# Up projections of a ConvGLU feed-forward: nine feature tiles by seven products instead of six, their weight sums loaded three and summed two tiles ahead, x's differences written earlier in the program

## Chip, cores and metric

The kernel runs on one core of one Trainium2 chip. The metric is the device time of one execution in microseconds (us). An execution was also recorded by the hardware profiler; times "at" a point below are microseconds from the start of that recorded span.

## What is computed

One encoder block on a sequence of 512 tokens with 1024 features. Three mixers (a bidirectional mLSTM, neighbourhood attention, cross-attention into a memory) are projected from a normed x, gated, merged and added to x. Then comes the feed-forward part, where the change lies:

```python
def conv_glu_ffn(h, w_up, w_conv, b_conv, w_down):
    a, u = jnp.split(h @ w_up, 2, axis=-1)
    return (jax.nn.gelu(dwconv3(a, w_conv, b_conv)) * u) @ w_down

x = x + merged @ w_out[l]
x = x + conv_glu_ffn(rms_norm(x, ffn_norm_g[l]), w_ffn_up[l], w_ffn_conv[l], b_ffn_conv[l], w_ffn_down[l])
return rms_norm(x, final_norm_g)
```

`D_FF` is 2816, so a and u have 22 feature tiles of 128 each. `dwconv3` is a convolution of three taps along the tokens.

## The kernel before

Features lie on the 128 partitions, tokens on the free axis. Every matmul of a float32 product is made of three in a rounded format: high part by high part, high by low, low by high (`mm3`, L370 to L372). So each weight block is split before use: ScalarE copies it into the rounded format (the high part, L336), VectorE subtracts that from it (the low part, L337). Blocks come in a fixed order: `emit_raw` (L246) loads them into a ring of three `wr` buffers from SP's queue, three blocks ahead, and the halves of a block are split one block ahead into four `w` buffers.

The stage before is the output projection: for each of 8 feature tiles an x tile is loaded (L1314, SP), 24 matmuls run, VectorE adds x (x2, L1316), ScalarE and VectorE split the scaled sum into `HH` and `HL`, ScalarE squares it (L1322), and GpSimd (POOL in the profile) adds the squares into `acc2` (L1323).

From `acc2` a chain makes `rb`, the row of reciprocal roots of the mean squares, on all partitions: a transposition on VectorE (L177), four stores of `td` to DRAM (L180), a load of `U` (L186), a sum and a scaling on VectorE (L202, L203), a power on POOL (L204), a small transposition (L205), four stores of `rd` (L208) and a broadcast load of `rb` (L210). Up to that point the up projections work on x2 without the root; `conv` (L570) multiplies tile after tile by `rb` first.

The up stage is a loop over f, 22 feature tiles:

- A plain tile makes a and u with two projections, `pa` and `pu`, of 24 matmuls of 512 columns each. Tiles 0 and 1 are run ahead of their convolutions; tile 1's results stand in the other pool of PSUM banks (`at`).
- A tile in `SUP` is made by seven products. With the tokens in two halves, the contraction tiles in even and odd, and the weights in a and u, a 2 by 2 block product needs eight products of half width; `up_seven` needs seven, each of 4 x 3 matmuls of 256 columns, in the order `UP_ORDER`. Their factors are blocks of x and of the weights or sums and differences of two (`FORMS`). The plain blocks come as one `ub` load; product 1's difference of weights is made on VectorE (L1383); for products 4, 7, 3 and 6 one addend is loaded into a `ut` buffer by SP (`up_load`, L1366) and the other is added to it in flight by a DMA from POOL's queue (`up_sum`, L1374). `up_weight` splits each of them (L1390, L1391).
- `x_forms(p)` makes the differences of x for one pair of contraction tiles: two copies on ScalarE (L1338), three subtractions on VectorE (L1341 to L1343), a split (L1345 to L1347). Its buffers y and d are single.

Behind the matmuls of a tile: multiplication by `rb` and the three taps (L570, L572 to L574), gelu on ScalarE (L1451), multiplication by `rb` again on POOL (`c`, L1453), and c times u on VectorE (L1467 or L1469). Tiles 0 to 11 end in `ur`, which the down projection uses in its own seven-product form; tiles 12 to 21 are split into `UH` and `UL`. In tiles 3 to 10, x2 is transposed and stored (`turn_out`), and in tiles 6 to 13 loaded back (`turn_in`) as the residual of the down projection.

A scheduler in the framework sets each engine's order of instructions from the written program, so an engine's order isn't the order of the text. `in_turn` chains an instruction behind the one before it on its engine. From an engine's queue instructions run in order; a DMA that waits for its buffer holds up those behind it in the same queue. The large buffers (`unit`, 14 of them), the small ones (`E`, six) and others are taken from pools when free.

## Time and profile before

| | |
|---|---|
| time, median of 3 runs | 851.85 us (851.35 to 852.55) |
| the profiled execution's own time | 851.33 us |
| its span | 849.6 us |
| granted TensorE clock, mean | 0.999 |
| busy: TensorE, its weight loads, VectorE, ScalarE, POOL | 841.0, 716.3, 622.4, 476.4, 175.6 us |
| moved by DMA | 147.32 MB, 173 GB/s |
| up projections | about 494.7 to 731.2 |
| tiles 2, 3, 4 / 5 / 6 / 7 start | 516.5, 527.4, 539.8 / 550.8 / 560.8 / 571.7 |
| down projections start | 731.2 |

PE is TensorE, PEld its weight loads, which run beside matmuls; DVE is VectorE, ACT ScalarE, SPq the queue of DMA issues on SP. A row of the order of time gives start, duration, engine, source line, operation and tiles (written <- read), and in brackets how long the engine stood idle before it and what ended that. Most waits of engines other than TensorE cost nothing by themselves.

### The profile page before, as it was taken

What the parts mean: (1) busy time and instruction counts of PE and PEld (TensorE: products, weight loads), DVE (VectorE), ACT (ScalarE), POOL (GpSimd) and SP (SyncE); (2) the same over time, 40 slices, a digit from 0 to 9 for tenths busy, and PEclk for the clock granted to TensorE, in tenths of its full rate; (3) what the DMA queues carried; (4) which work ended last, traced back from release to release, by engine and by line L of the source; (5) the groups of instructions that cost most, each with busy time, mean ns of one, the idle gap of its engine ahead of it and who ended that gap; (6) DMA issues with size and microseconds to landing.
All of it is one profiled execution on the core that took longest, in us unless ns stands there. A gap on an engine that the chain in (4) does not pass through costs nothing.

```text
span 849.6 us, 12743 instructions
## 1 busy us (share of the span) xinstructions
PE 841.0 (99%) x4214; PEld 716.3 (84%) x4214; DVE 622.4 (73%) x1246; ACT 476.4 (56%) x992; POOL 175.6 (21%) x268
## 2 busy tenths in 40 slices
PE   9999999999999999999999999999999999999997
PEld 8898988888888888888888888799999888888885
DVE  6699777766458748998676666877777856687893
ACT  7465557775446548888644644444455544444562
POOL 2000200000101840454000121423332111320421
PEclk9999999999999999999999999999999999999999
DMA  8236736563425856788743343588886333895882
GB/s 273 84 114 202 246 120 205 168 198 102 145 90 172 229 145 199 223 250 234 232 140 109 117 159 99 132 235 226 224 229 147 101 109 124 234 231 143 250 197 99
DMA packets 86226, 147.32 MB, mean 173 GB/s; under 512 B 11784, under 2 KB 38920, under 8 KB 86160
## 3 DMA queue, kind: packets, MB, share of 16 engines
q1 hardware_dynamic: 71600, 127.47, 46.9%
q0 software_dynamic: 14272, 18.90, 12.2%
q8 instruction: 33, 0.54, 0.3%
q14 instruction: 33, 0.27, 0.1%
q10 hardware_dynamic: 288, 0.14, 0.1%
HBM read 130.84 MB, written 15.62 MB: 172 GB/s over the span
## 4 chain that ended last, share of the span: by engine, by line
PE 91%; DMA 3%; DVE 2%; issue 2%; ACT 1%; POOL 0%; SPq 0%; POOLq 0%; DVEq 0%; ACTq 0%
PE mm L372 23%; PE mm L370 23%; PE mm L371 23%; PE at L372 6%; PE at L371 6%; PE at L370 6%; DMA s<-xT 2%; PE at L1033 1%; PE at L866 1%; PE at L868 1%; PE at L850 1%; DVE w L337 1%; PE at L404 0%; PE at L999 0%; PE at L1000 0%
## 5 line engine op out<-in xcount | busy, mean ns | idle before, releaser
L370 PE MATMUL mm<-u,w 128*128 128x512 f32 x763 | 298.8, 392 | 0.0
L372 PE MATMUL mm<-u,w 128*128 128x512 f32 x763 | 297.5, 390 | 1.0 <-DVE w L337 1.0
L371 PE MATMUL mm<-u,w 128*128 128x512 f32 x763 | 297.5, 390 | 0.0
L337 DVE TENSOR_TENSOR w<-wr,w 128x512 fp32r<-128x512 f32 (+2 forms) x233 | 159.8, 690 | 69.9 <-ACT w L336 68.5
L336 ACT ACTIVATE w<-wr 128x512 fp32r<-128x512 f32 (+2 forms) x232 | 144.8, 627 | 113.0 <-PE mm L372 72.2
L372 PEld LDWEIGHTS mm<-u,w 128*128 128x128 f32 x763 | 143.4, 188 | 32.0 <-DVE w L337 1.8
L371 PEld LDWEIGHTS mm<-u,w 128*128 128x128 f32 x763 | 143.5, 188 | 28.6
L370 PEld LDWEIGHTS mm<-u,w 128*128 128x128 f32 x763 | 143.5, 188 | 28.5
L679 POOL DMA_DIRECT2D u<-nav_d x128 | 62.3, 505 | 99.8 <-PE at L1033 52.3
L270 POOL TENSOR_TENSOR s<-s,rb 128x512 f32<-128x512 f32 x21 | 31.1, 1480 | 154.4 <-ACT s L1451 151.0
L372 PE MATMUL at<-u,w 128*128 128x256 f32 (+1 forms) x200 | 60.2, 301 | 0.0
L371 PE MATMUL at<-u,w 128*128 128x256 f32 (+1 forms) x200 | 60.0, 300 | 0.0
L370 PE MATMUL at<-u,w 128*128 128x256 f32 (+1 forms) x200 | 60.0, 300 | 0.0
L270 ACT ACTIVATE w<-u 128x512 fp32r<-128x512 f32 x52 | 32.7, 632 | 41.5 <-PE mm L372 20.6
L370 PE MATMUL mm<-w,u 128*128 128x512 f32 x128 | 50.4, 394 | 0.0
L372 PE MATMUL mm<-w,u 128*128 128x512 f32 x128 | 49.9, 390 | 0.0
L371 PE MATMUL mm<-w,u 128*128 128x512 f32 x128 | 49.9, 390 | 0.0
L270 DVE TENSOR_TENSOR w<-u,w 128x512 fp32r<-128x512 f32 x52 | 35.7, 688 | 18.1 <-ACT w L270 17.5
L572 ACT ACTIVATE s<-pad,vec 128x512 f32<-128x512 f32 x30 | 24.3, 812 | 27.6 <-DVE pad L570 24.3
L371 PEld LDWEIGHTS at<-u,w 128*128 128x128 f32 x200 | 38.2, 191 | 1.5
L370 PEld LDWEIGHTS at<-u,w 128*128 128x128 f32 x200 | 38.2, 191 | 1.5
L372 PEld LDWEIGHTS at<-u,w 128*128 128x128 f32 x200 | 38.2, 191 | 1.3
(333 smaller groups left out, 1390.3 us busy)
## 6 DMA issues: line engine op xcount, KB each, us to landing
wr<-wflat SPq DMA_DIRECT2D x118, 512.0 KB, 3.7
u<-wflat SPq DMA_DIRECT2D x50, 256.0 KB, 5.7
td<-s SPq DMA_DIRECT2D x172, 64.0 KB, 1.9
U<-td SPq DMA_DIRECT2D x41, 256.0 KB, 4.0
s<-xT SPq DMA_DIRECT2D x24, 256.0 KB, 4.0
ut<-wflat SPq DMA_DIRECT2D x24, 256.0 KB, 4.3
ut<-wflat POOLq DMA_DIRECT2D x24, 256.0 KB, 7.3
u<-wflat POOLq DMA_DIRECT2D x24, 256.0 KB, 7.6
```

The source lines that it names most:

```text
L270: chain[eng] = getattr({"V": V, "A": A, "G": G}[eng], what)(*a, **k).ins
L336: A.activation(h[:, u:v], src, AF.Copy)
L337: V.tensor_tensor(l[:, u:v], src, h[:, u:v].bitcast(F32), op=ALU.subtract)
L370: PE.matmul(ps, lh, rh, start=start, stop=False)
L371: PE.matmul(ps, lh, rl, start=False, stop=False)
L372: st["mm"] = PE.matmul(ps, ll, rh, start=False, stop=stop).ins
L572: A.activation(t1, pad[:, 0:512], AF.Identity, scale=vcol(w, i), bias=vcol(b, i))
L679: G.dma_start(vw[r * 32:(r + 1) * 32, i * 256:(i + 1) * 256], nav_v[hf, r, CW[b]:CW[b] + 32, hp * 256:(hp + 1) * 256])
L850: PE.matmul(pv[:, i, 0:129], kt[:, d, i], va[:, i + d, h, 0:129], start=True, stop=True)
L866: PE.matmul(pv[:, d, 0:129], E[J // 2][:, 2 * (J % 2) + d, :], va[:, J, h, 0:129], start=True, stop=not inter)
L868: PE.matmul(pv[:, d, 0:129], Q[d][:, i, :], C[:, d, i, 0:129], start=False, stop=True)
L1033: PE.matmul(py[:, bl * 256:(bl + 1) * 256], vw[:, c:c + P], pp[bl][:, hf * 256:(hf + 1) * 256], start=hf == 0, stop=hf == 1)
```

## The change

Tiles 3, 17 and 19 join `SUP`. `up_load` runs three tiles ahead (tile 3's own at tile 0), `up_sum` two tiles ahead (tile 3's behind rb's chain in the text). The last of the four `ut` buffers comes from another tag, so six `E` buffers hold two tiles' sums. Products 7, 3 and 6 write banks of the `mm` pool. `x_forms` is written ahead: block 0 inside the output projection, 1 to 3 between tiles 0 and 1. The residual's way back moves from tiles 6 to 13 into tiles 20 and 21, into `unit` buffers; tiles 12 to 15 put `UH` and `UL` into the buffers that it leaves. `in_turn` covers the power of rb's chain, rb's load and the `ut` loads too.

```diff
-SUP = (5, 7, 9, 11, 13, 15)
+SUP = (3, 5, 7, 9, 11, 13, 15, 17, 19)
...
-        G.tensor_tensor(col[:, :NT], v, nhalf[:, :NT], op=ALU.pow)
+        in_turn("G", "tensor_tensor", col[:, :NT], v, nhalf[:, :NT], op=ALU.pow)
...
-        SY.dma_start(rb, d.partition_broadcast(P))
+        in_turn("S", "dma_start", rb, d.partition_broadcast(P))
...
     def x_forms(p):
 
+        for q in (p, 4):
+            if q not in xf:
+                xf[q] = unit(F32R)
...
+    for f in range(KT):
+        xr = scr()
+        chain["S"] = SY.dma_start(xr, xT[:, f, :]).ins
+        ps = proj(("out", f), GH, GL)
...
+            chain["G"] = G.tensor_tensor(acc2, acc2, sq, op=ALU.add).ins
+        if f == 3:
+            x_forms(0)
...
-                r = tp.tile([P, S], F32, tag="E", name=nm("ut"), bufs=EB)
-                SY.dma_start(r, src[:, :HC])
+                tag, n = ("nab", 2) if i == 6 else ("E", EB)
+                r = tp.tile([P, S], F32, tag=tag, name=nm("ut"), bufs=n)
+                in_turn("S", "dma_start", r, src[:, :HC])
...
-        b12, b45, b7, b36 = [atps() for _ in range(4)]
+        b12, b45, b7, b36 = atps(), atps(), mmps(), mmps()
...
         if f == 0:
+            up_load(SUP[0])
...
             t2 = turn_in(turn_out(by4(acc2)), "nab", 2)
+            x_forms(1)
...
             pa1 = proj(("ua", 1), HH, HL, bank=atps)
+            x_forms(2)
             rb2 = rstd_row_turned(t2, "2")
+            up_sum(SUP[0])
+            x_forms(3)
             pu1 = proj(("uu", 1), HH, HL, bank=atps)
         elif f in SUP:
+            if f + 2 in SUP:
+                up_sum(f + 2)
             pa, pu = up_seven(f)
         else:
-            if f + 1 in SUP:
-                up_sum(f + 1)
             pa = pa1 if f == 1 else proj(("ua", f), HH, HL)
-        if f + 2 in SUP:
-            up_load(f + 2)
+        if f + 3 in SUP[1:]:
+            up_load(f + 3)
...
-        if f < KT // 2:
-            x_forms(f)
...
-            if f % 2 == 0:
-                ou.append(unit(F32R))
...
+            if f < 2 * NSP + 4:
+                for tag, part in zip("HR", (UH, UL)):
+                    part.append(tp.tile([P, S], F32R, tag=tag, name=nm("UH"), bufs=4))
...
-        if 6 <= f < 14:
-            t, g = (f - 6) % NT, (f - 6) // NT
-            res[t, g] = turn_in(turns[t, g], "HR"[g], 4)
+        if f >= FT - 2:
+            g, u = FT - 1 - f, unit()
+            for t in range(NT):
+                q = u[:, t * S:(t + 1) * S]
+                SY.dma_start(q, turns[t, g])
+                res[t, g] = q.rearrange("p (i s a) -> p s i a", i=4, a=32)
```

VectorE around tile 2's convolution, before. `pad_150` and `s_5565` belong to tile 2, `u_5336` is d of `x_forms`, `w_5584` the second half of tile 3's first weights, `u_5335` holds products c times u:

```order
L573 SCALAR_TENSOR_TENSOR s_5565<-pad_150,vec,s_5565 128x512
L1346 TENSOR_TENSOR u_5339<-u_5336,u_5339 128x768
L1347 TENSOR_TENSOR u_5342<-u_5336,u_5339 128x512
L574 SCALAR_TENSOR_TENSOR s_5565<-pad_150,vec,s_5565 128x512
L1341 TENSOR_TENSOR u_5336<-u_5337 128x512
L1342 TENSOR_TENSOR u_5336<-u_5337 128x512
L1343 TENSOR_TENSOR u_5336<-u_5337 128x256
L337 TENSOR_TENSOR w_5584<-wr_5466,w_5584 128x512
L1467 TENSOR_TENSOR u_5335<-mm_5587,s_5565 128x512
```

The same place now. `s_5601` is tile 2's convolution, `wr_5510` tile 3's block of plain weights, `s_5609` the difference for its first product, `w_5611` and `w_5614` its first two splits, `ut_5348` a sum:

```order
L570 TENSOR_TENSOR pad_150<-mm_5567,rb_5495 128x512
L1390 TENSOR_TENSOR s_5609<-wr_5510 128x512
L1478 TENSOR_TENSOR u_5347<-mm_5373,s_5544 128x512
L1478 TENSOR_TENSOR u_5347<-at_5518,s_5552 128x512
L573 SCALAR_TENSOR_TENSOR s_5601<-pad_150,vec,s_5601 128x512
L1398 TENSOR_TENSOR w_5611<-s_5609,w_5611 128x512
L574 SCALAR_TENSOR_TENSOR s_5601<-pad_150,vec,s_5601 128x512
L1398 TENSOR_TENSOR w_5614<-wr_5510,w_5614 128x512
L1398 TENSOR_TENSOR w_5653<-ut_5348,w_5653 128x512
```

No difference of x stands there any more; the splits of tile 3's first products do.

VectorE between the transposition of `acc2` (L177, two rows above the first one here) and rb's scaling (L203), now; `u_5009` is d, `w` rows are splits, L202 is rb's sum. Before, only L202 and four splits stood between L177 and L203:

```order
L1328 TENSOR_TENSOR u_5009<-u_5010 128x256
L1331 TENSOR_TENSOR u_5473<-u_5009,u_5473 128x768
L1332 TENSOR_TENSOR u_5174<-u_5009,u_5473 128x512
L1326 TENSOR_TENSOR u_5009<-u_5010 128x512
L337 TENSOR_TENSOR w_5369<-wr_5308,w_5369 128x512
L1327 TENSOR_TENSOR u_5009<-u_5010 128x512
L1328 TENSOR_TENSOR u_5009<-u_5010 128x256
L337 TENSOR_TENSOR w_5442<-wr_5356,w_5442 128x512
L202 TENSOR_REDUCE y_5482<-U_5423 128x4
L1331 TENSOR_TENSOR u_5501<-u_5009,u_5501 128x768
L337 TENSOR_TENSOR w_5445<-wr_5356,w_5445 128x512
L203 TENSOR_SCALAR y_5482<-y_5482 128x4
```

Blocks 2 and 3 of the differences moved in here.

POOL behind the power of rb's chain (L204), before: four multiplications c times rb (tiles 0 to 3), then the sums of tile 5:

```order
L204 TENSOR_TENSOR y_5452<-y_5451,nhalf 128x4
L1453 TENSOR_TENSOR s_5500<-s_5500,rb_5464 128x512
L270 TENSOR_TENSOR s_5516<-s_5516,rb_5464 128x512
L270 TENSOR_TENSOR s_5565<-s_5565,rb_5464 128x512
L270 TENSOR_TENSOR s_5655<-s_5655,rb_5464 128x512
L270 DMA ut_5646<-wflat 128x512
```

and now, the power being the first row (`ut_5348` to `ut_5354` are tile 3's):

```order
L270 TENSOR_TENSOR y_5483<-y_5482,nhalf 128x4
L270 DMA ut_5348<-wflat 128x512
L270 DMA ut_5350<-wflat 128x512
L270 DMA ut_5352<-wflat 128x512
L270 DMA ut_5354<-wflat 128x512
L270 TENSOR_TENSOR s_5544<-s_5544,rb_5495 128x512
```

The sums of tile 3 moved between the power and the first multiplication.

More of the change, by code (lines that the diff above doesn't have):

```diff
@@ L269, in in_turn @@
         with tc.issue_after(chain[eng]) if eng in chain else ExitStack():
-            chain[eng] = getattr({"V": V, "A": A, "G": G}[eng], what)(*a, **k).ins
+            chain[eng] = getattr({"V": V, "A": A, "G": G, "S": SY}[eng], what)(*a, **k).ins
     def emit_sum(i):
@@ L1347, in x_forms @@
         V.tensor_tensor(xf[4][:, p * S:(p + 1) * S], d[:, 3 * M:], h[:, 3 * M:].bitcast(F32), op=ALU.subtract)
+    for f in range(KT):
+        xr = scr()
+        chain["S"] = SY.dma_start(xr, xT[:, f, :]).ins
+        ps = proj(("out", f), GH, GL)
+        V.tensor_tensor(x2[f], ps, xr, op=ALU.add)
+        split_act(HH[f], HL[f], x2[f], vcol("ffn_g", f))
+        if f == 0:
+            A.activation(acc2, x2[f], AF.Square)
+        else:
+            sq = scr()
+            A.activation(sq, x2[f], AF.Square)
+            chain["G"] = G.tensor_tensor(acc2, acc2, sq, op=ALU.add).ins
+        if f == 3:
+            x_forms(0)
+    x2v = [u[:, :4 * S].rearrange("p (f s) -> p f s", f=4) for u in x2u]
+    ur[0] = unit()
+    ur.extend(unit() for _ in range(NSP // 2 - 3))
+    ou, UH, UL = [], [], []
+    res, turns = {}, {}
     def x_of(i, p):
@@ L1392, in up_weight, with up_first @@
         uw[f, "w", i] = h, l
+    def up_first(f):
+        uw[f] = split.pop(BINDEX["ub", f][0])
+        for n in range(2):
+            up_weight(f, n)
     def up_seven(f):
-        b12, b45, b7, b36 = [atps() for _ in range(4)]
+        b12, b45, b7, b36 = atps(), atps(), mmps(), mmps()
         at = {1: b12[:, :M], 2: b12[:, M:], 4: b45[:, :M], 5: b45[:, M:], 7: b7[:, :M], 3: b36[:, :M], 6: b36[:, M:]}
@@ L1460, in hybrid_block @@
                 ws = weights(("uu", f))
-                uw[f + 1] = split.pop(BINDEX["ub", f + 1][0])
-                for n in range(2):
-                    up_weight(f + 1, n)
+                up_first(f + 1)
                 split[BINDEX["uu", f][0]] = ws
```

36 lines of the change are left out of this document (10 added, 26 removed).

## The prediction

> **What bounds the kernel now.** I read the page first (busy shares, then the chain that ended last), and after that the order of time on TensorE through the up projections, with a table by stretch.
>
> ```profile
> span 849.6 us, 12743 instructions
> PE 841.0 (99%) x4214; PEld 716.3 (84%) x4214; DVE 622.4 (73%) x1246; ACT 476.4 (56%) x992; POOL 175.6 (21%) x268
> ...
> PE 91%; DMA 3%; DVE 2%; issue 2%; ACT 1%; POOL 0%; SPq 0%; POOLq 0%; DVEq 0%; ACTq 0%
> ```
>
> TensorE carries 91% of the chain. So the time changes by what TensorE has to issue, plus the places where it waits. Busy time does not show the first, since matmuls overlap; the distance from one start to the next does. These rows of the order of time are the first matmul of up tile 2 (516.48), a pause in tile 3, and the first matmuls of tiles 5, 6, 7 and 8. Columns: start, duration, engine, line.
>
> ```profile
> 516.48 0.39 PE L370 MATMUL mm<-u,w 128*128 128x512 f32 x1
> ...
> 530.30 0.39 PE L371 MATMUL mm<-u,w 128*128 128x512 f32 x1
> 531.74 0.50 PE L372 MATMUL mm<-u,w 128*128 128x512 f32 x1 [1.05 <-DVE w L337]
> ...
> 550.76 0.28 PE L370 MATMUL at<-u,w 128*128 128x256 f32 x1
> 560.84 0.40 PE L370 MATMUL mm<-u,w 128*128 128x512 f32 x1
> 571.74 0.28 PE L370 MATMUL at<-u,w 128*128 128x256 f32 x1
> 581.82 0.40 PE L370 MATMUL mm<-u,w 128*128 128x512 f32 x1
> ```
>
> A plain tile (6) takes 571.74 - 560.84 = 10.90 us for 48 matmuls of 512 columns, 0.227 us each. A tile by seven products (7) takes 581.82 - 571.74 = 10.08 us for 84 matmuls of 256 columns, 0.120 us each. The difference is only 0.82 us: seven products save an eighth of the columns, and shorter matmuls give more than a third of that back.
>
> ```profile
> 560.84:571.74 10.90, 10.90 (x50) 9.01 (x49) 8.88 (x15) 3.66 (x6) 5.14 (x5) 1.00 0.83 229
> 571.74:581.82 10.08, 10.08 (x85) 10.07 (x84) 7.58 (x14) 6.62 (x13) 1.30 (x1) 1.00 1.02 278
> 665.90:731.20 65.30, 65.30 (x290) 54.09 (x289) 42.65 (x63) 29.16 (x46) 8.73 (x7) 1.00 0.39 128
> ```
>
> By stretch (columns: stretch, length, then busy time and count of PE, PEld, DVE, ACT, POOL, the granted clock, DMA share, GB/s), the six plain tiles 16 to 21 take 65.30/6 = 10.88 us each, so the plain tile's price holds late too. VectorE is busy 16.5 us of a pair's 20.98 and DMA over 0.8: both are near their limits, but neither stops TensorE in these rows.
>
> **The change, part by part.**
>
> *Three more tiles by seven products (3, 17, 19).* 3 x 0.82 = 2.46 by the pair above; with 10.88 for the plain tile 2.40. I take **-2.4**. Moving two of the four banks to the other pool changes no matmul; tile 2's and 4's banks come free at their convolution and product, long before the fifth product asks. VectorE and ScalarE take on what the pair above shows them carrying without a stop, so this work costs nothing there; if that cover were gone, each split that is late would cost its own 0.7 us.
>
> *A rule that speaks against it.*
>
> ```profile
> L370 PEld LDWEIGHTS mm<-u,w 128*128 128x128 f32 x232 | 43.6, 188 | 8.9
> ...
> L370 PEld LDWEIGHTS at<-u,w 128*128 128x128 f32 x184 | 35.2, 191 | 0.8
> ```
>
> A seven-product tile has 84 weight loads of 191 ns against 48 of 188, and its loads leave no idle time (0.8 us in 184). If they could not run beside matmuls, 84 x 0.191 = 16.0 us of loads against 48 x 0.188 = 9.0 would make such a tile 16.0 - 9.0 = 7.0 us dearer in loads alone. The starts 0.120 us apart say that they do overlap. The Trainium skill, "TensorE: Matmul & The Clock Gate", section "What overlaps and what doesn't" under "The mechanism", says that a load overlaps running matmuls only where the row groups differ; this trace disagrees, and I keep it as a rival of one chance in a hundred.
>
> *The pause in tiles 2 to 4 goes.* From 516.48 to 550.76 are 34.28 us for three plain tiles of 10.90, so 1.58 us are lost, nearly all at 531.74. There TensorE waits for the low half of tile 3's weights (L337), which VectorE makes late:
>
> ```profile
> 529.47 0.68 DVE L1341 TENSOR_TENSOR u<-u 128x512 f32<-128x512 f32 x1
> 530.07 0.68 DVE L1342 TENSOR_TENSOR u<-u 128x512 f32<-128x512 f32 x1
> 530.67 0.41 DVE L1343 TENSOR_TENSOR u<-u 128x256 f32<-128x256 f32 x1
> 531.00 0.68 DVE L337 TENSOR_TENSOR w<-wr,w 128x512 fp32r<-128x512 f32 x1
> ```
>
> Three differences of x stand right ahead of it. In the changed order all four blocks of differences stand ahead of the first convolution, and this split does not exist any more. **-1.6**.
>
> *What is late next: the first weights of tile 3.* Seven products now start where tile 3 started, at 516.48 + 2 x 10.90 = 527.38, and its third matmul (527.6) needs the low half of the block's own difference. Its place on VectorE is behind the convolutions of tiles 0, 1 and 2, and these begin only when the row of reciprocal roots (rb) has landed:
>
> ```profile
> 518.46 0.69 DVE L570 TENSOR_TENSOR pad<-mm,rb 128x512 f32<-128x512 f32 x1 [3.15 <-DMA rb<-rd]
> ...
> 526.06 0.69 DVE L1467 TENSOR_TENSOR u<-at,s 128x512 f32<-128x512 f32 x1 [0.57 <-POOL s L270]
> 526.67 0.74 DVE L573 SCALAR_TENSOR_TENSOR s<-pad,vec,s 128x512 f32<-128x512 f32 x1
> 527.33 0.95 DVE L1346 TENSOR_TENSOR u<-u,u 128x768 fp32r<-128x768 f32 x1
> 528.20 0.68 DVE L1347 TENSOR_TENSOR u<-u,u 128x512 fp32r<-128x512 f32 x1
> ```
>
> As many VectorE rows stand between that L570 and tile 2's L573 as before, so the latter comes 526.67 - 518.46 = 8.2 us after rb; the split follows 0.66 us later (L573's distance to the row behind it, 527.33) and takes 0.68. It ends at rb + 9.5. So **TensorE waits (rb's landing - 518.1)**. With rb as before that is 0.4 us. Where does rb land?
>
> ```profile
> 499.79 1.30 POOL L1323 TENSOR_TENSOR acc<-acc,s 128x512 f32<-128x512 f32 x1 [4.06 <-ACT s L1322]
> 501.12 0.71 DVE L177 STREAM_TRANSPOSE s<-acc 128x512 f32<-128x512 f32 x1 [1.21 <-POOL acc L1323]
> 507.86 0.69 DVE L202 TENSOR_REDUCE y<-U 128x4 f32<-128x512 f32 x1 [1.39 <-DMA U<-td]
> 509.07 0.16 DVE L203 TENSOR_SCALAR y<-y 128x4 f32<-128x4 f32 x1
> 510.62 1.31 SPq L208 DMA_DIRECT2D rd<-y  x4
> 515.11 0.34 SPq L210 DMA_DIRECT2D rb<-rd  x1
> ```
>
> This chain starts at the last output tile, which waits for its x (loaded by SP at 494.03), and that load stands behind a weight load that waits for VectorE:
>
> ```profile
> 492.30 0.68 DVE L1316 TENSOR_TENSOR u<-mm,s 128x512 f32<-128x512 f32 x1
> 492.90 0.67 DVE L337 TENSOR_TENSOR w<-wr,w 128x512 fp32r<-128x512 f32 x1
> 494.03 0.37 SPq L1314 DMA_DIRECT2D s<-xT  x1
> 497.67 0.69 DVE L1316 TENSOR_TENSOR u<-mm,s 128x512 f32<-128x512 f32 x1 [1.39 <-PE mm L372]
> ```
>
> Differences prepared sooner take rows from in front of 492.30. Stepping through the new order from the fourth output tile on with 3.6 us from an x load's issue to use (494.03 to 497.67) and 1.3 us of VectorE behind each sum, the last one comes at 495.3, 2.4 us sooner. Half of that goes again: between transposition and L202 there are now nine rows of differences and splits, about 5.1 us at their distances in the rows above, and some 1.2 us of waiting for ScalarE, so L202 is not at 505.5 but at about 506.1; and one more row of differences (0.87, from L1346 to L1347 above) stands between L202 and L203. Net rb 0.9 us sooner.
>
> Against it: the four weight sums of tile 3 now stand on POOL directly behind the power (L204), so their 1 MB moves while rd and rb do. No row shows rb beside sums. The nearest are the small writes td beside them (first row, 540 to 560) and with less of them (585 to 607), median us to landing last:
>
> ```profile
> td<-s SPq DMA_DIRECT2D x8, 64.0 KB, 6.8
> ...
> td<-s SPq DMA_DIRECT2D x11, 64.0 KB, 1.8
> ```
>
> That is 0 to 5.0 us; a gain is excluded, since nothing is taken from these queues. rd has 0.5 KB and rb 256 KB, the four td 256 KB in far smaller pieces, so I take 2.0, under half. Then rb lands at 518.46 - 0.9 + 2.0 = 519.6 and the wait is **+1.5**; its ends are 0 (no contention) and 4.5 (5.0). The Trainium skill, "DMA: Bandwidth & Descriptors", section "Queues, rings and completion order", says that a DMA engine takes turns between queues packet by packet. By that rule rb meets at most as much foreign data as it has itself, 256 KB, about 1 us at the 260 GB/s that the table below shows, and the wait would be 0.5; the td row went beyond such a share, so I do not lower the sum.
>
> *Loads three and sums two tiles ahead.* ScalarE's waits for sums cost TensorE nothing in the trace, so their end is worth 0. On POOL the four issues pass one multiplication each; c is due a product later, 0 again.
>
> *x2's way back (2 MB) moves from tiles 6 to 13 into tiles 20 and 21,* on SP ahead of late raw weights.
>
> ```profile
> U<-td SPq DMA_DIRECT2D x41, 256.0 KB, 4.0
> ...
> 710.00:715.00 5.00, 5.00 (x24) 4.14 (x23) 2.67 (x4) 1.61 (x3) 0.32 (x1) 1.00 0.18 52
> 735.00:740.00 5.00, 5.00 (x24) 4.14 (x23) 2.81 (x5) 2.21 (x4) 1.78 (x2) 1.00 1.07 254
> ...
> 742.19 0.63 ACT L270 ACTIVATE w<-u 128x512 fp32r<-128x512 f32 x1 [1.99 <-DMA u<-wflat]
> ```
>
> At 254 GB/s the 2.1 MB take 8 us, and the DMA share of 0.18 at 710 has room, but four raw blocks move from about 720 to 730, into a stretch that is full (1.07), where ScalarE already waits 1.99 us. TensorE reaches that block, the tenth of the down projection, behind seven sums of 6 matmuls and two plain blocks of 12, at 731.2 + 66 x 0.227 = 746.2; its split is done some 1.3 us after 742.19, so 2.7 us are to spare. I take **0**; the ends are 0 and 4.
>
> **Sum**, against the profiled execution's own 851.33 (span 849.6): 851.33 - 2.4 - 1.6 + 1.5 = 848.8. The median of the runs is 851.85, 0.5 above, so **849.4**.
>
> **Rivals.**
> - *No wait at tile 3:* rb sooner, or sums that do not slow it. 848.8 - 1.5 + 0.5 = 847.8. For it: the two DMAs are small. Chance 0.17, faster.
> - *A new wait for the one removed:* rb 0.8 to 4.2 us later than I take it, a wait of 2.3 to 5.7 us, 850.2 to 853.5. For it: the td row's 5.0. 0.21, same.
> - *Slower by that one mechanism:* it decides where the wait passes 4.0 + 1.7 = 5.7 us, that is where rb lands after 523.8, 6.2 us of contention against the chain's own sooner start. At 6.5 us of wait 854.4. For it: both rd and rb pass beside sums, one after the other; against it their size. 0.06.
> - *The down projection starts short of weights:* 1 to 3.5 us, about 851.9, same, 0.07; over 4 us, 853.8, slower, 0.04. For it the 1.07; against it that the 2.7 us to spare.
> - *It does nothing* (tiles held by VectorE, 16.5 us of 20.98): 851.85, 0.02. *Weight loads bind:* three tiles 7.0 us dearer instead of 0.8 cheaper, 849.4 + 2.4 + 21 = about 873, 0.01.
>
> **How the numbers follow.** The forecast (wait 0.7 to 2.3 us) has 0.42. 0.2% of 851.85 is 1.7 us, about what a measurement tells from no change, so faster means below 850.15 and slower above 853.55. Faster 0.42 + 0.17 = 0.59; same 0.21 + 0.07 + 0.02 = 0.30; slower 0.06 + 0.04 + 0.01 = 0.11. The range, 847.4 to 852.8, leaves out the slower cases and the ends of the best and the late one. The forecast's own range is 848.5 to 850.2.
>
> **What would show it.** Nine tiles of 10.1 us on TensorE; no pause of 1.4 us within 48 matmuls of 512 columns; a pause of about 1.5 us at the third matmul of tile 3, ended by VectorE's split; L570 first at about 519.6, with rd and rb slower than 3.3 us to land. I am wrong if rb lands before 518 or after 521, if TensorE stops between tile 4 and 21, or if it stops between 731 and 760 for a split that waited for a DMA.

## The result and the profile after

| | before | after |
|---|---|---|
| median of 20 runs each, us | 851.84 (850.27 to 853.25) | 853.52 (852.47 to 855.02) |
| profiled execution, us (its span) | 851.33 (849.6) | 853.43 (851.7) |
| mean granted TensorE clock in it | 0.999 | 0.995 |

The ratio is 1.0021, with a 95% interval of 1.0015 to 1.0028: the change costs 1.3 to 2.4 us. Predicted were 849.4, with a range of 847.4 to 852.8.

The first page of after, its span, its busy times and the shares of the chain of work that ended last:

```profile
span 851.7 us, 13056 instructions
...
PE 839.9 (99%) x4322; PEld 720.2 (85%) x4322; DVE 640.5 (75%) x1276; ACT 484.5 (57%) x1010; POOL 187.7 (22%) x280
...
PE 92%; DMA 3%; issue 2%; DVE 1%; POOL 1%; ACT 0%; SPq 0%; POOLq 0%; DVEq 0%; ACTq 0%
```

Nothing on it looks wrong. TensorE is even busy 1.1 us less than before, and the time is 2 us longer. That can only be idle time or a stretch at another rate, so I looked for it in the order of time on TensorE (start, duration, engine, line): the first matmul of tile 2, the last of tile 2, the first three of tile 3, the first of tile 4 and the first of tile 5.

```profile
515.76 0.39 PE L370 MATMUL mm<-u,w 128*128 128x512 f32 x1
...
526.68 0.39 PE L372 MATMUL mm<-u,w 128*128 128x512 f32 x1
529.80 0.58 PE L370 MATMUL at<-u,w 128*128 128x256 f32 x1 [2.74 <-ACT w L1397]
530.18 0.42 PE L371 MATMUL at<-u,w 128*128 128x256 f32 x1
532.18 0.58 PE L372 MATMUL at<-u,w 128*128 128x256 f32 x1 [1.58 <-DVE w L1398]
...
544.00 0.40 PE L370 MATMUL mm<-u,w 128*128 128x512 f32 x1
...
554.91 0.28 PE L370 MATMUL at<-u,w 128*128 128x256 f32 x1
```

All of the loss lies in tile 3. From 515.76 to 544.00 are 28.24 us for two tiles that need 10.91 + 10.07 = 20.98 by the table below; 7.3 us are lost. Tile 2 ends at 526.9, so the third matmul of tile 3, the first that needs the low half of its weights (L1398), was due at 526.9 + 2 x 0.12 = 527.15 and came 5.0 us later. Another 2.0 are rate: 82 matmuls from 532.18 to 544.00 take 11.82 us, 0.144 each, where 0.120 each would take 9.84. (The last 0.25 are lost within tile 2.) The table by stretch (length, busy time and count of PE, PEld, DVE, ACT and POOL, then granted clock, DMA share, GB/s) says why:

```profile
528.00:530.00 2.00, 0.20 (x1) 0.20 (x2) 1.60 (x2) 1.44 (x3) 2.00 (x2) 0.92 0.00 0
530.00:532.00 2.00, 0.60 (x2) 0.30 (x2) 1.82 (x3) 0.79 (x2) 0.14 (x1) 0.50 0.00 0
532.00:534.00 2.00, 1.82 (x8) 1.82 (x9) 1.99 (x4) 1.15 (x2) 0.47 (x1) 0.50 0.00 0
534.00:536.00 2.00, 2.00 (x12) 2.00 (x11) 1.99 (x2) 0.63 (x1) 2.00 (x3) 0.50 0.40 127
536.00:538.00 2.00, 2.00 (x16) 2.00 (x16) 0.96 (x3) 0.98 (x3) 2.00 (x3) 0.87 0.62 95
538.00:540.00 2.00, 2.00 (x19) 2.00 (x18) 1.70 (x3) 1.15 (x3) 0.67 (x1) 1.00 1.06 245
```

The granted clock halves 2.6 us after tile 2's last matmul has ended (527.07; from the share of 0.92 it falls at 529.7), and it is still at half when TensorE has work again: 12 matmuls in two microseconds instead of 19. Before had a stop of 1.05 us at this place, and its clock stayed up.

Everywhere else the kernel does what was expected of it. The same table over the start of the down projection, a plain tile and a tile by seven products:

```profile
733.60:760.00 26.40, 26.40 (x118) 21.84 (x117) 19.43 (x31) 14.05 (x23) 9.06 (x11) 1.00 0.98 270
544.00:554.91 10.91, 10.91 (x50) 9.02 (x49) 9.49 (x16) 4.87 (x8) 2.29 (x2) 1.00 0.74 217
554.91:564.98 10.07, 10.07 (x85) 10.07 (x84) 7.38 (x13) 5.68 (x11) 4.45 (x5) 1.00 0.82 181
```

What is tile 3 late for? VectorE's rows (the first multiplication by rb, and the low half of tile 3's first weights), SP's and POOL's issues, and the transfers between 505 and 525 (the queues' share of 16 engines; issues with KB each and median us to landing):

```profile
522.56 0.69 DVE L570 TENSOR_TENSOR pad<-mm,rb 128x512 f32<-128x512 f32 x1 [7.97 <-DMA rb<-rd]
...
531.44 0.68 DVE L1398 TENSOR_TENSOR w<-s,w 128x512 fp32r<-128x512 f32 x1
```

```profile
511.27 3.57 POOL L270 DMA_DIRECT2D ut<-wflat  x4
```

```profile
511.58 1.31 SPq L208 DMA_DIRECT2D rd<-y  x4
512.93 0.36 SPq L246 DMA_DIRECT2D wr<-wflat  x1
515.27 0.34 SPq L270 DMA_DIRECT2D rb<-rd  x1
515.66 2.46 SPq L270 DMA_DIRECT2D ut<-wflat  x4
```

```profile
q1 hardware_dynamic: 1292, 3.09, 46.4%
q0 software_dynamic: 576, 1.05, 32.2%
...
ut<-wflat POOLq DMA_DIRECT2D x4, 256.0 KB, 9.0
ut<-wflat SPq DMA_DIRECT2D x4, 256.0 KB, 8.6
rb<-rd SPq DMA_DIRECT2D x1, 256.0 KB, 7.3
```

rb needs 7.3 us where before it landed 518.46 - 515.11 = 3.35 us after its issue, and VectorE waits for it for 7.97 us. The split then ends 9.6 us behind rb. The raw weight block issued on SP ahead of rb (512.93) is late as well: it takes 7.6 us to land, at 520.5.

### The profile page after: what moved, and what is told of

Read it like the earlier page. It is cut to its first block, busy times and chain, and to the rows that moved or that the text cites. A ratio compares the mean times of both kernels' runs of the same rounds, so it can differ in the third digit from the quotient of the medians.

```text
span 851.7 us, 13056 instructions
## 1 busy us (share of the span) xinstructions
PE 839.9 (99%) x4322; PEld 720.2 (85%) x4322; DVE 640.5 (75%) x1276; ACT 484.5 (57%) x1010; POOL 187.7 (22%) x280
## 4 chain that ended last, share of the span: by engine, by line
PE 92%; DMA 3%; issue 2%; DVE 1%; POOL 1%; ACT 0%; SPq 0%; POOLq 0%; DVEq 0%; ACTq 0%
PE mm L370 23%; PE mm L371 23%; PE mm L372 23%; PE at L372 6%; PE at L371 5%; PE at L370 5%; PE at L1033 1%; DMA s<-xT 1%; DMA rb<-rd 1%; PE at L866 1%; PE at L868 1%; PE at L850 1%; DMA ut<-wflat 1%; PE at L999 0%; PE at L1000 0%
## 5 line engine op out<-in xcount | busy, mean ns | idle before, releaser
L370 PE MATMUL mm<-u,w 128*128 128x512 f32 (+1 forms) x823 | 310.5, 377 | 0.0
L372 PE MATMUL mm<-u,w 128*128 128x512 f32 (+1 forms) x823 | 309.2, 376 | 0.0
L371 PE MATMUL mm<-u,w 128*128 128x512 f32 (+1 forms) x823 | 309.2, 376 | 0.0
L337 DVE TENSOR_TENSOR w<-wr,w 128x512 fp32r<-128x512 f32 (+2 forms) x221 | 151.0, 689 | 57.4 <-ACT w L336 55.8
L336 ACT ACTIVATE w<-wr 128x512 fp32r<-128x512 f32 (+2 forms) x220 | 137.1, 626 | 83.1 <-PE mm L372 54.3
L372 PEld LDWEIGHTS mm<-u,w 128*128 128x128 f32 x823 | 155.0, 188 | 28.4 <-DVE w L337 0.4
L371 PEld LDWEIGHTS mm<-u,w 128*128 128x128 f32 x823 | 155.1, 188 | 26.6
L370 PEld LDWEIGHTS mm<-u,w 128*128 128x128 f32 x823 | 155.1, 188 | 26.5
L270 POOL TENSOR_TENSOR s<-s,rb 128x512 f32<-128x512 f32 x22 | 33.2, 1512 | 157.6 <-ACT s L1469 157.6
L370 PE MATMUL at<-u,w 128*128 128x256 f32 (+1 forms) x176 | 54.3, 309 | 2.7 <-ACT w L1397 2.7
L372 PE MATMUL at<-u,w 128*128 128x256 f32 (+1 forms) x176 | 54.3, 308 | 1.6 <-DVE w L1398 1.6
L371 PE MATMUL at<-u,w 128*128 128x256 f32 (+1 forms) x176 | 54.1, 308 | 0.0
L370 PEld LDWEIGHTS at<-u,w 128*128 128x128 f32 x176 | 34.7, 197 | 4.7 <-ACT w L1397 3.2
L370 PE MATMUL mm<-w,u 128*128 128x512 f32 x96 | 37.8, 394 | 0.0
L372 PE MATMUL mm<-w,u 128*128 128x512 f32 x96 | 37.4, 390 | 0.0
L371 PE MATMUL mm<-w,u 128*128 128x512 f32 x96 | 37.4, 389 | 0.0
L372 PEld LDWEIGHTS at<-u,w 128*128 128x128 f32 x176 | 34.5, 196 | 3.1 <-DVE w L1398 1.9
L371 PEld LDWEIGHTS at<-u,w 128*128 128x128 f32 x176 | 34.6, 197 | 1.6
```

Source lines behind the costliest of these rows:

```text
L270: chain[eng] = getattr({"V": V, "A": A, "G": G, "S": SY}[eng], what)(*a, **k).ins
L336: A.activation(h[:, u:v], src, AF.Copy)
L337: V.tensor_tensor(l[:, u:v], src, h[:, u:v].bitcast(F32), op=ALU.subtract)
L370: PE.matmul(ps, lh, rh, start=start, stop=False)
L371: PE.matmul(ps, lh, rl, start=False, stop=False)
L372: st["mm"] = PE.matmul(ps, ll, rh, start=False, stop=stop).ins
```

## The experiments

Three theories. **A**: POOL's four sums of tile 3 (software queue, 1 MB), which move at the same time as rd and rb, make rb late; the first weights of tile 3 stand behind the convolutions on VectorE and are late with it. **B**: tile 5's four loads, issued right behind rb on the same queue, make it late. **C**: rb is not decisive; VectorE has too much to do there. And one question of size: how much of the loss is the clock?

Each kernel was timed beside before on the same chip, and the differences below are ratios times 851.8. Edits are against the changed kernel unless another is named.

**1. Tile 3's loads and sums moved into the output projection** (the two functions are defined earlier for it).

```diff
     for f in range(KT):
...
+        if f == 0:
+            up_load(SUP[0])
+        if f == 4:
+            up_sum(SUP[0])
...
         if f == 0:
-            up_load(SUP[0])
...
-            up_sum(SUP[0])
             x_forms(3)
```

> Tile 3's loads and POOL's four sums move from beside rb to the output projection; the four loads of tile 5 stay right behind rb on SP. Theory A (POOL's sums slow rb): rb lands 3.4 us after its issue instead of 7.3, TensorE waits at most 1 us at tile 3, the granted clock stays at 1.00, time 847.5 to 848.5. Theory B (the loads behind rb slow it): rb still takes about 7 us and the time stays at 853.5. Theory C (VectorE's added work makes the weights late whatever rb does): rb may land sooner, the first split of tile 3 still ends near 532, time 853 or so.

Measured: 854.86 us, ratio 1.0036 (1.0024 to 1.0049). rb's own time fell, from 7.3 to 5.1 us, but rb landed no sooner, at 523.02. The reason is the same collision at another place: the sums now move beside an x load of the output projection. In this kernel that x load was issued at 486.44, and VectorE got it at

```profile
494.13 0.69 DVE L1357 TENSOR_TENSOR u<-mm,s 128x512 f32<-128x512 f32 x1 [5.47 <-DMA s<-xT]
```

7.7 us later; in after the same load was issued at 485.55 and used at

```profile
489.86 0.69 DVE L1338 TENSOR_TENSOR u<-mm,s 128x512 f32<-128x512 f32 x1 [2.08 <-DMA s<-xT]
```

4.3 us later. The chain to rb begins at those x, so the time that rb won was lost ahead of it; TensorE, too, began tile 2 only at 517.98, where after began it at 515.76. As a test of the time A's expectation failed; as a sight of the mechanism it is a second case of it. B's expectation (rb still 7 us) fell too, but 5.1 is not 3.35 either. C's came true in its numbers (the first split ended at 532.6), but since rb landed as late as before, this run can't tell C from A.

**2. Tile 3 plain again**, eight tiles by seven products, x's differences early as in after, tile 5's loads behind rb.

```diff
-SUP = (3, 5, 7, 9, 11, 13, 15, 17, 19)
+SUP = (5, 7, 9, 11, 13, 15, 17, 19)
...
-            up_load(SUP[0])
...
-            up_sum(SUP[0])
             x_forms(3)
...
+            if f == 3:
+                up_sum(f + 2)
             pa = pa1 if f == 1 else proj(("ua", f), HH, HL)
-        if f + 3 in SUP[1:]:
+        if f + 3 in SUP:
             up_load(f + 3)
```

> Tile 3 is computed as a plain tile again (eight tiles by seven products), so its four loads, four sums and the weights that TensorE waited for are gone; x's differences stay early, and tile 5's loads stay right behind rb. A: rb takes 3.4 us, no pause in tiles 2 to 4 and the clock stays at 1.00: 851.84 - 1.6 (two tiles) - 1.6 (the old pause) = 848.6, a little less for the earlier start. B: rb takes about 7 us, and the convolutions behind it are late by 3 to 4 us; the plain tiles do not wait for them in VectorE's order until their own splits, so 849 to 852. C: VectorE's rows make the split of the plain tile 3 late, about 851.

Measured: 848.32 us, ratio 0.9956 (0.9943 to 0.9969), against the 848.6 worked out. There is no stop in tiles 2 to 4. rb took 5.4 us without any sums, so the loads behind it do slow it, by less than the sums.

**3. Filling the idle time.** Forty matmuls on constant data between tiles 2 and 3; nobody reads their output.

```diff
+            if f == 3:
+                pw3 = atps()
+                with tc.issue_after(st["mm"]):
+                    for _ in range(40):
+                        PE.matmul(pw3[:, :256], warm[:, :P], warm, start=True, stop=True)
             pa, pu = up_seven(f)
```

> The kernel of after with 40 matmuls of 256 columns on constant data between tiles 2 and 3, 4.8 us of TensorE's time within its wait, whose output nobody reads. All theories leave rb and the weights as late as before. If the halved clock behind the idle time is 2 us of the loss of 7.3, the clock stays at 1.00 and the time is 853.5 - 2.0 = 851.5; if the wait alone is the loss and the low clock costs nothing (TensorE would have waited again for the next splits), 853.5.

Measured: 852.37 us, ratio 1.0003 (0.9994 to 1.0011), that is 1.5 us less than after by the ratios. In its order of time the fill, the first three matmuls of tile 3 and the first of tile 4:

```profile
528.38 4.96 PE L1467 MATMUL at<-warm 128*128 128x256 f32 x40
533.18 0.28 PE L370 MATMUL at<-u,w 128*128 128x256 f32 x1
533.30 0.28 PE L371 MATMUL at<-u,w 128*128 128x256 f32 x1
533.72 0.38 PE L372 MATMUL at<-u,w 128*128 128x256 f32 x1
...
543.65 0.40 PE L370 MATMUL mm<-u,w 128*128 128x512 f32 x1
```

and the stretch that stood at half clock in after:

```profile
534.00:536.00 2.00, 2.00 (x19) 2.00 (x19) 1.99 (x4) 1.64 (x3) 0.93 (x1) 1.00 0.00 0
```

The weights come 1.5 us later than in after (rb landed at 524.04), and yet tile 4 starts 0.35 us sooner: 82 matmuls take 9.93 us instead of 11.82. The halved clock is 1.9 us of the loss in after's profiled execution; the other 5 us are nearly all the wait. Useless work in the gap made the kernel faster than after.

**4. Tile 5's loads behind the next raw block**, its sums a tile later; tile 3's sums stay beside rb.

```diff
-            if f + 2 in SUP:
+            if f + 2 in SUP[2:]:
                 up_sum(f + 2)
...
+            if f == 4:
+                up_sum(f + 1)
             pa = pa1 if f == 1 else proj(("ua", f), HH, HL)
-        if f + 3 in SUP[1:]:
+        if f + 3 in SUP[2:]:
             up_load(f + 3)
+        if f == 3:
+            chain["S"] = st["wr"]
+            up_load(f + 2)
```

(`st["wr"]` is the last raw block's load.)

> The kernel of after with tile 5's four loads queued on SP behind the next raw weight block instead of right behind rb (issued about 524.5 instead of 515.7), and its sums one tile later on POOL; tile 3's sums stay where they are, beside rb. A: rb still takes about 7 us, 853.5. B: rb takes 3.4 us, TensorE waits 0.5 us or less, 848 to 849. If both slow it, rb lands in between, near 5 us, and the time is 850 to 852.

Measured: 853.91 us, ratio 1.0022 (1.0011 to 1.0034), the same as after, and

```profile
rb<-rd SPq DMA_DIRECT2D x1, 256.0 KB, 7.3
```

as in after. B falls as the cause: with the sums there, taking the loads away changes nothing.

**5. Tile 3's four sums left out.**

```diff
-            up_sum(SUP[0])
+            for i in UP_ORDER:
+                if (SUP[0], i) in uw:
+                    uw[SUP[0], i] = uw[SUP[0], i][0]
             x_forms(3)
```

> The kernel of after without the four sums of tile 3 on POOL: its four summed weights are left as the first halves, so tile 3 is computed from other weights with the same instructions. Nothing else moves. A: rb's issue about 513.9 and 5.3 us to land, TensorE waits about 2 us, the clock stays up: 848.3. If the sums cost nothing: 853.5.

Measured: 848.63 us, ratio 0.9968 (0.9957 to 0.9980). rb took 5.2 us and landed at 518.90, TensorE stopped for 0.8 us, the clock stayed up. This is A's forecast to 0.3 us. With nothing moved and only the sums gone, the whole loss goes. VectorE's rows are the same as in after, so C alone does not explain the loss either.

**6. The sums held until rb has landed**, by one small POOL instruction that reads rb ahead of them.

```diff
+            in_turn("G", "tensor_tensor", tiny(1), rb2[:, :1], nhalf[:, :1], op=ALU.mult)
             up_sum(SUP[0])
             x_forms(3)
```

> The kernel of after with one small POOL instruction that reads rb put ahead of tile 3's four sums, so that these start moving only when rb has landed. A (sums beside rd and rb make rb late): rd to rb's issue takes 2.3 us instead of 3.7, rb 5.3 us instead of 7.3 as in the run with tile 3 plain, so it lands about 519.2; the low half of tile 3's first weights is done 9.6 us later and TensorE waits about 2 us without a drop of the clock: 853.5 - 3.3 - 1.9 = 848.3, if the sums, some 8 us later now, are there when their splits ask; if they are not, 849 to 852. If the loads behind rb are what makes it late, rb stays at 7 us and the time at 853.5.

Measured: 848.58 us, ratio 0.9968 (0.9955 to 0.9980). One instruction turns a loss of 1.8 us into a gain of 2.7, with everything computed. The order of time of POOL shows it (POOL reads rb, issues the sums, and goes on to the multiplications by rb):

```profile
518.97 0.19 POOL L270 TENSOR_TENSOR y<-rb,nhalf 128x1 f32<-128x1 f32 x1 [7.48 <-DMA rb<-rd]
519.72 3.63 POOL L270 DMA_DIRECT2D ut<-wflat  x4 [0.56 <-DMA ut<-wflat]
523.55 3.02 POOL L270 TENSOR_TENSOR s<-s,rb 128x512 f32<-128x512 f32 x2 [0.20 <-ACT s L1470]
```

The sums 8 us later are still in time for their splits; what is left on TensorE is one stop of 1.03 us at tile 3's third matmul.

**7. Both out of rb's way:** experiment 6 with experiment 4's loads.

```diff
+            in_turn("G", "tensor_tensor", tiny(1), rb2[:, :1], nhalf[:, :1], op=ALU.mult)
             up_sum(SUP[0])
...
+        if f == 3:
+            chain["S"] = st["wr"]
+            up_load(f + 2)
```

> The run with the sums held until rb has landed (848.6), with tile 5's four loads also queued on SP behind the next raw block, so that nothing of tiles 3 and 5 moves beside rb. A and B together (the loads add the 1.9 us between 3.35 and 5.2): rb lands 3.4 us after its issue, near 517.5, the first weights of tile 3 are in time and the remaining stop of 1.3 us goes: 847.2. If rb is not made slower by the loads behind it, 848.6 stays.

Measured: 846.66 us, ratio 0.9944 (0.9931 to 0.9956): faster than before by 4.8 us, and than after by 6.6 by the ratios, the fastest of all kernels here. The transfers from 505 to 525, VectorE's rows for rb and for the first low half, and tile 3 by stretch:

```profile
rb<-rd SPq DMA_DIRECT2D x1, 256.0 KB, 3.8
```

```profile
518.06 0.69 DVE L570 TENSOR_TENSOR pad<-mm,rb 128x512 f32<-128x512 f32 x1 [2.44 <-DMA rb<-rd]
...
527.02 0.68 DVE L1398 TENSOR_TENSOR w<-s,w 128x512 fp32r<-128x512 f32 x1
```

```profile
527.66:537.73 10.07, 10.07 (x86) 10.07 (x84) 9.95 (x17) 6.09 (x12) 1.62 (x1) 1.00 0.88 266
```

The split ends at 527.70, and TensorE asks for it at 527.9. Tile 3 takes its 10.07 us without a stop. The loads did count once the sums were gone: 3.8 against 4.9 us for rb.

**8. Six tiles by seven products as before**, the rest as in experiment 2 (edit against it).

```diff
-SUP = (5, 7, 9, 11, 13, 15, 17, 19)
+SUP = (5, 7, 9, 11, 13, 15)
```

> The kernel of after with the six feature tiles of before by seven products (5 to 15), x's differences sooner and the loads three tiles ahead as in after. By the terms of the prediction it has the 1.6 of the old pause and nothing else: 852.1 - 1.6 = 850.5, ratio 0.998, and the run with eight tiles stands two tiles of 0.82 below it. If the gain of that run came from the two tiles alone or the pause alone, this one stands at 852.1 or at 848.3.

Measured: 849.64 us, ratio 0.9977 (0.9968 to 0.9986), or 2.0 us (1.2 to 2.7) for the old pause alone; 1.6 was its term. The eight tiles of experiment 2 stand 1.6 us below it by the spans of their profiles (847.7 and 846.1): 0.8 a tile.

**9. Tile 3's first two weights prepared ahead of the convolutions** in program order; sums and loads stay beside rb.

```diff
             pu1 = proj(("uu", 1), HH, HL, bank=atps)
+            pa2 = proj(("ua", 2), HH, HL)
+            ws = weights(("uu", 2))
+            up_first(3)
+            split[BINDEX["uu", 2][0]] = ws
...
-            pa = pa1 if f == 1 else proj(("ua", f), HH, HL)
+            pa = pa1 if f == 1 else pa2 if f == 2 else proj(("ua", f), HH, HL)
...
-            if f + 1 in SUP:
+            if f > 2 and f + 1 in SUP:
                 ws = weights(("uu", f))
```

> The kernel of after with the first two weights of tile 3 prepared in front of the three convolutions in program order, so that on VectorE their low halves stand some 4 rows behind the first multiplication by rb instead of 10 and more; sums and loads stay beside rb. If the loss is a late rb with the weights queued behind it on VectorE: rb still takes about 7 us, the low half of the first weights is done about 4 us after it instead of 9.6, near 527, TensorE waits 0.5 us or less and the clock stays up: 853.5 - 4.8 - 1.9 = 846.8. If TensorE lacks rb's products for another reason (banks, later splits), 850 to 853.

Measured: 852.60 us, ratio 1.0016 (1.0008 to 1.0025). The second forecast. The first low half came 4.6 us behind rb as wanted, and tile 3 began without a wait; but it then stopped five times, idle for 0.2 to 1.7 us each, and took 15.4 us instead of 10.07. VectorE's rows behind rb (products of tiles 0 to 2 are L1482, low halves L1398) show the second bottleneck:

```profile
522.75 0.69 DVE L570 TENSOR_TENSOR pad<-mm,rb 128x512 f32<-128x512 f32 x1 [7.54 <-DMA rb<-rd]
...
526.67 0.69 DVE L1398 TENSOR_TENSOR w<-s,w 128x512 fp32r<-128x512 f32 x1
...
529.38 0.69 DVE L1482 TENSOR_TENSOR u<-mm,s 128x512 f32<-128x512 f32 x1 [0.76 <-POOL s L270]
...
535.70 0.69 DVE L1482 TENSOR_TENSOR u<-mm,s 128x512 f32<-128x512 f32 x1 [2.05 <-POOL s L270]
536.31 0.68 DVE L1398 TENSOR_TENSOR w<-wr,w 128x512 fp32r<-128x512 f32 x1
```

The later splits queue behind products that wait for POOL's multiplication by rb. So the debt of a late rb, three tiles of convolutions and products, stood ahead of most of tile 3's splits in this order too. C holds to this extent: VectorE's backlog is the path from rb to the stop. In the profiled execution the clock stayed at 1.00 through these five short stops, with 4.1 us of idle time in all (after's two stops had 2.74 + 1.58 = 4.3). It need not have done so in the others: in 5 of the 12 the mean granted clock was 0.996, and before's executions have 0.997 to 0.999. The stretches of the profiled one:

```profile
528.00:530.00 2.00, 1.36 (x10) 0.95 (x8) 1.24 (x4) 1.95 (x4) 1.95 (x2) 1.00 0.00 0
530.00:532.00 2.00, 0.82 (x7) 0.82 (x8) 2.00 (x4) 0.43 (x1) 0.58 (x1) 1.00 0.00 0
...
534.00:536.00 2.00, 1.00 (x7) 0.60 (x5) 0.30 (x1) 2.00 (x5) 1.60 (x2) 1.00 0.40 131
```

**10. The sums ahead of the power on POOL**, so that they move beside the earlier links of the chain (td, U).

```diff
+            up_sum(SUP[0])
             t2 = turn_in(turn_out(by4(acc2)), "nab", 2)
...
             rb2 = rstd_row_turned(t2, "2")
-            up_sum(SUP[0])
             x_forms(3)
```

> The kernel of after with tile 3's four sums ahead of the power on POOL instead of behind it, so that they start some 11 us sooner and move beside td and U, the earlier two steps of the same chain to rb, and no longer beside rd and rb. A, that sums slow whatever plain transfer runs beside them (rb took 7.3 instead of 5.1 us, an x load in the run with sums in the output projection 7.7 instead of 4.3): U lands 3 to 5 us later, rd and rb are 3.4 us faster together, so rb lands at 522 to 524 as before and the time is 853 to 855. If td and U pass the sums unharmed, rb lands about 519.2 and the time is 848.5.

Measured: 854.11 us, ratio 1.0031 (1.0019 to 1.0043). From 499 to 513 the four td took

```profile
td<-s SPq DMA_DIRECT2D x4, 64.0 KB, 6.5
```

against 1.8 in after, rb landed at 523.69 and TensorE stopped about as long as in after. A's forecast held for td, the link that the sums moved beside; U, which was issued just behind the last sum's landing, took 2.4 us, much as in after (2.5).

**11. Late rb without tile 3 by seven products:** experiment 2 with four loads and sums that nobody uses at the places of tile 3's.

```diff
+            up_load(5)
             wa, wu = weights(("ua", f)), weights(("uu", f))
...
             rb2 = rstd_row_turned(t2, "2")
+            up_sum(5)
```

> The run with tile 3 plain (848.3), to which four loads and four sums are added at the places that tile 3's had in after (tile 5's first summed weights, loaded and summed a first time into tiles that nobody reads; their proper loads and sums follow as they did). A: rb takes 7.3 us and lands at 522 to 523, and TensorE loses nothing or under 1 us by it, since a plain tile 3 has its weights split ahead of the convolutions: 848.3 to 849.3. If a late rb alone costs what after lost, 853 to 854.

Measured: 850.88 us, ratio 0.9989 (0.9980 to 0.9997), 2.8 us above experiment 2. I had expected under 1. rb took 7.3 us, and the plain tile 3 stopped too, once:

```profile
533.13 0.50 PE L372 MATMUL mm<-u,w 128*128 128x512 f32 x1 [1.40 <-DVE w L337]
```

By the profiles 2.0 us are lost in tile 3, which takes 12.9 us (528.11 to 541.01) where experiment 2's takes 10.9; most of the rest lies ahead of tile 2, which begins 0.8 us later than there. So a late rb costs about 2.0 us with a plain tile 3, and some 7 in after, halved clock included, where tile 3 is computed by seven products.

**12. The even tiles, 4 to 20**, by seven products: nine tiles, the first a tile later (edit against experiment 2).

```diff
-SUP = (5, 7, 9, 11, 13, 15, 17, 19)
+SUP = (4, 6, 8, 10, 12, 14, 16, 18, 20)
...
-            if f == 3:
+            if f == 2:
                 up_sum(f + 2)
```

> Nine tiles by seven products as in after, but the even ones 4 to 20, so that the first comes a tile later and its sums are issued on POOL behind the first two multiplications by rb. A: no stop at tile 4, the clock stays up; one more tile of 0.82 than in the run with eight: 848.3 - 0.8 = 847.5. If VectorE's work at the first such tile is what stops TensorE, or tile 20 delays the first weights of the down projection, 849 or more.

Measured: 851.08 us, ratio 0.9995 (0.9986 to 1.0004), 3.6 above what I expected. Tile 4 began without a stop and took 10.07 us, as A has it. The loss is at the other end, at the start of the down projection: ScalarE waits for a raw weight block, TensorE stops 2.3 us for ScalarE, and the clock falls again (ScalarE's row, then TensorE's stretch with DMA at 1.05 to 1.10 of its engines). Tile 20's work and x2's way back meet there; which of them holds up the block was not tried.

```profile
734.27 0.63 ACT L270 ACTIVATE w<-wr 128x512 fp32r<-128x512 f32 x1 [2.93 <-DMA wr<-wflat]
```

```profile
732.00:734.00 2.00, 0.62 (x3) 0.19 (x1) 0.07 (x1) 0.00 (x0) 0.00 (x0) 1.00 1.05 404
734.00:736.00 2.00, 1.04 (x3) 0.86 (x4) 1.07 (x2) 1.63 (x3) 1.52 (x2) 0.67 1.10 333
```

That is the rival "the down projection starts short of weights" of the prediction, which after itself escaped.

The runs with nine tiles that start at 3 beside each other, but for experiment 9, whose order on VectorE is another. The distance from rb's landing (first L570) to tile 3's third matmul is the same to 0.1 us wherever TensorE waited. With experiments 5 to 7, which moved rb's landing and nothing that this matmul reads, that makes the landing the cause of the stop and not a companion:

| run | rb in transfer, us | rb lands | behind tile 2's first matmul | third matmul of tile 3 | behind rb | ratio to before |
|---|---|---|---|---|---|---|
| after | 7.3 | 522.56 | 6.80 | 532.18 | 9.62 | 1.0021 |
| 4, loads later | 7.3 | 524.42 | 6.70 | 534.04 | 9.62 | 1.0022 |
| 3, fill | 7.5 | 524.04 | 7.21 | 533.72 | 9.68 | 1.0003 |
| 1, sums in the output projection | 5.1 | 523.02 | 5.04 | 532.67 | 9.65 | 1.0036 |
| 10, sums ahead of the power | 4.8 | 523.69 | 6.44 | 533.30 | 9.61 | 1.0031 |
| 6, sums after rb | 4.9 | 518.92 | 2.62 | 528.61 | 9.69 | 0.9968 |
| 5, no sums | 5.2 | 518.90 | 2.35 | 528.58 | 9.68 | 0.9968 |
| 7, both after rb | 3.8 | 518.06 | 1.28 | 527.89 | no wait | 0.9944 |

## Why the prediction was wrong

- **Three tiles, -2.4: right.** 10.91 - 10.07 = 0.84 each in after, 0.8 between experiments 2 and 8. Seven products never bound TensorE by their weight loads; VectorE carried them in every tile but the first.
- **The old pause, -1.6: right,** 2.0 (1.2 to 2.7) in experiment 8.
- **The wait at tile 3, +1.5: this step failed,** and in one term of it, the contention of rd and rb with the sums. The formula held: the low half ends at rb + 9.6 (I had 9.5). The wait came as two stops, though: 2.74 us at tile 3's first matmul, for the high half from ScalarE, which I had not placed, and 1.58 at the third, where I had put all of it. The chain to rb came out nearly as I had it, but by luck and not by my steps: without neighbours rb lands 1.28 us behind tile 2's first matmul (experiment 7), against 518.46 - 516.48 = 1.98 before, 0.7 sooner where I had 0.9. rd was in fact issued later than before (511.58 against 510.62), since VectorE's new rows between the transposition and L203 took more than the gain; but rd to rb's issue took 2.2 us in experiment 7, where it had taken 515.11 - 510.62 = 4.5 before. What held it up before is not shown.
- **The contention, which I took at 2.0 with an upper end of 5.0, is 5.0 to 5.5.** From rd's issue to rb's landing pass 522.56 - 511.58 = 10.98 us in after and 518.06 - 512.05 = 6.01 in experiment 7, 5.0 less: rd to rb's issue took 3.7 and 2.2, rb itself 7.3 and 3.8. Counted from tile 2's first matmul, as in the table, it is 5.5 (6.80 - 1.28) with sums and loads, 5.4 (6.70 - 1.28) with the sums alone and 1.1 (2.35 - 1.28) with the loads behind rb alone. The row of td beside sums that I had quoted, 6.8 against 1.8 us, was nearly the answer; I discounted it by more than half since rb moves in larger pieces, and no row supported that discount. Rather, rd and rb are two transfers, one after the other, and both meet the sums. I had also not counted tile 5's loads, which the same change puts right behind rb.
- With rb's landing as it was, 6.80 behind tile 2's first matmul, rb lands at 516.48 + 6.80 = 523.3 on the clock of before, and the formula gives a wait of 5.2; 5.0 was measured. That is just short of the 523.8 from which I had called it slower.
- **The clock was missing.** No term of mine lets TensorE run slower after a stop; by experiment 3 that is 1.9 us in the profiled executions and 1.5 us by the ratios, and without it the median of 853.5 would have been near 852, within my range. Its size changes from one execution to the next: 11 of after's 20 have a mean granted clock of 0.994 or 0.995, 9 have 0.997, and the 11 took 1.0 us longer on average. The Trainium skill, "TensorE: Matmul & The Clock Gate", section "What's actually happening", tells of half clock after one idle window of about 3.4 us, on a window that runs free. The length of the window agrees with the traces: the half clock lasted 6.8 us in after (shares 0.92, 0.50, 0.50, 0.50 and 0.87 of five stretches of 2 us) and 3.4 us in experiment 12 (0.67, 0.50 and 0.98). That the window has to be idle throughout does not agree. In after the clock fell 2.6 us after the last matmul's end; in experiment 1, with two stops of 1.27 and 1.88 us close together, it fell only when TensorE had resumed (at 532.67; the clock stood at 1.00 until 534 and at 0.51 from 534 to 536).
- **The estimate of 1 us by the Trainium skill's rule of turns between queues,** "DMA: Bandwidth & Descriptors", section "Queues, rings and completion order", failed: rb alone took 3.9 us longer than before. (The table that I named has 254 GB/s where I wrote 260, which changes nothing.) The rule itself is not refuted by that. My estimate let rb meet as many bytes as it has itself; it left out the raw block of 512 KB that stands ahead of rb on SP's queue, and that a sum's byte costs the DMA engines more (last section).
- The terms add up. For the profiled executions -2.4 - 1.6 + 5.0 + 2.0 (the rate) + 0.25 (within tile 2) - 0.7 is about +2.5, and the down projection starts 733.6 - 731.2 = 2.4 us later. The -0.7 is tile 2's start, 515.76 against 516.48, for which I had no term; experiments 2, 5 and 6 begin tile 2 at 516.3 to 516.6, so it is no gain of the change.
- **The loads and sums ahead, and x2's way back, 0: right** in after, where TensorE does not stop at the start of the down projection. But the room there was thin: in experiment 12, with the last tile by seven products one later, TensorE stopped for 2.3 us.

The likeliest rival, a new wait for the one removed, was the right one, at the long end of what I allowed it (5.0 of 2.3 to 5.7 us), and with the halved clock besides.

## What to carry to other kernels

Before a bulk transfer is put at a new place, look at which small transfers stand on the path there, and price them with the worst row in which the two were seen together, every link of the chain by itself. When a transfer is to be early but not too early, a single small instruction that reads the small transfer's result, queued ahead of the bulk one, was enough here. And a stop of TensorE of 2 to 3 us can have a second price behind it, the halved clock, so that even useless matmuls in it can pay.

## What the runs showed of the hardware

- Four accumulating transfers of 256 KB on POOL's queue slowed each transfer of SP that was looked at beside them: rb 7.3 us instead of 3.8, an x load of 256 KB 7.7 instead of 4.3, four td of 64 KB 6.5 instead of 1.8, a raw block of 512 KB 7.6 (in after and in experiment 1) instead of 3.3 (in experiment 7). That block stood just ahead of rb and of the x load in SP's queue, and landed 2.0 and 0.4 us before them. How much of their delay is their own, and how much is the block's, was not told apart.
- Four or five plain loads of the same size, issued on SP just behind rb, cost it 1.1 to 2.2 us (4.9 to 6.0 in experiments 2, 5, 6, 8 and 12 against 3.8), and nothing in addition once the sums were there (7.3 with and without).
- A sum's byte held the DMA engines twice as long as one of SP's. By the two queue rows of after (20 us of 16 engines) the sums took 0.322 x 320 / 1.05 = 98 us of an engine for each MB, SP's transfers 0.464 x 320 / 3.09 = 48. Why it does was not tried.
- The granted clock fell to 0.50 within 2.6 us of the last matmul in after, and came back 6.8 us after it fell (529.7 to 536.5, from the shares 0.92 and 0.87 of two stretches), of which some 4.3 were worked. It also fell in a stop of 2.3 us (experiment 12) and behind stops of 1.27 and 1.88 us (experiment 1). Single stops of 1.0 to 1.4 us (before, experiments 6 and 11) left it at 1.00, and so did the five of experiment 9, all in the profiled executions.
